# Two attention output projections as seven products of 2x2 blocks, with the tokens on the array's side

## The chip, the cores and the metric

The kernel runs on one NeuronCore of a Trainium2 chip. TensorE (PE) multiplies: a matmul holds a block of 128 x 128 as array weights and streams columns of the other operand through it, at most 512 here. VectorE (DVE), ScalarE (ACT) and GpSimd (POOL) do the elementwise work, SyncE (SP) starts most transfers. Each engine runs its own instructions in order and waits on semaphores for the others. The metric is the device time of one execution in microseconds (us).

## The reference, cut to what matters

A trunk of two layers on 512 tokens of width 1024, all in float32. Layer 0 attends with 8 latent heads of width 128, layer 1 with 16 heads of width 64 over a chunked band; each layer ends with an output projection by a matrix of 1024 x 1024, a norm, a residual sum, and a SwiGLU feed-forward network (FFN).

```python
for layer in range(DEPTH):
    h = rms_norm(x, attn_pre_g[layer])
    y = mla_mixer(h, ...) if layer < N_A_LAYERS else chunked_mixer(h, k_band, v_band, ...)   # each ends: return o @ w_o
    x = x + rms_norm(y, attn_post_g[layer])
    h = rms_norm(x, ffn_pre_g[layer])
    f = swiglu(h, ffn_w_gate[layer], ffn_w_up[layer], ffn_w_down[layer])
    x = x + rms_norm(f, ffn_post_g[layer])
```

`rms_norm(y, g)` is `y * rsqrt(mean(y*y) + 1e-6) * g` over the 1024 features.

## The kernel before

**Layout and precision.** Activations are stored with features on the 128 partitions and the 512 tokens along the row, eight such tiles for width 1024. Each float32 operand is split into a high and a low part: ScalarE casts the high part, VectorE subtracts it to get the low part (`split`, profile lines L144 and L145; with a gain L148 and L149). One product then takes three matmuls: high by high, and the two mixed ones (`mm3`, L352 to L354). In most stages the weights are the array's side and tokens are the moving columns.

**Weights.** `Feed` holds a plan of all weight tiles in order of use. `feed.next` hands out a tile of 1024 columns already split, and keeps up to two later tiles loading through SyncE's queue and splitting. Raw tiles lie in a ring of 5, split tiles (`whi`, `wlo`) in rings of 3; some tiles have rooms of their own (`wh`).

**Attention and what is woven in.** `attention` walks slots of one head and one quarter of the queries. A `Filler` steps a generator of other TensorE work in between, at a rate set by the count `units`; its last part is `out_first`, the first two groups of the output projection, whose last step (k = 7) has to wait for the last head. A head ends when the row sums' reciprocal is spread over the partitions by TensorE (`bc`) and VectorE divides the head (`of`), which is then split (`oh`, `ol`).

**Output projection before.** `out_proj` makes 4 groups of two output blocks over k = 0..7, with W_o as the array's side and the heads as moving columns. Two groups are the woven ones (512 columns), the last two run by halves of 256 tokens, so that the first half's norm can start early. `Post` collects the norm: ScalarE keeps `y` with the gain (L559) and squares, VectorE adds the squares (`acc`), TensorE transposes them (`tot`, L431) for the sums, GpSimd takes the power -1/2 (L448), TensorE spreads the result (`bc`, L465), VectorE multiplies (L597) and adds into `x` (L599). Right behind it `ffn` starts gate/up by token halves (`half`, 256 columns, `b<-xh,whi`).

**Seven products that exist already.** The FFN's down projection (`Down`, `Hidden`, `down`, `After`) is computed with tokens on the array's side and 512 columns of W_down moving (L1169). Tokens, hidden blocks and output columns are each cut in two, and the four blocks of the product come from seven products of sums of blocks, named A11, A22, A12, E1, E2, E3, E6, in place of eight. VectorE or an accumulating DMA of GpSimd's queue (L250) makes the weight sums, VectorE the sums of hidden blocks. Since tokens are then on the partitions, `After` turns the result: ScalarE copies or VectorE adds each product into `y` (L1218, L1223), ScalarE squares with a row sum (L1228), GpSimd takes the power (L1263), ScalarE scales the rows (L1271), TensorE transposes (`yt`, L1291), VectorE adds into `x` with the gain (L1294). After each half of the output columns, `turn(0)` or `turn(1)` does this for the half of the tokens that is whole.

Of the kernel before, what the change touches and what calls it, by code (L numbers as in the profile page):

```python
# [68 lines left out]
def trunk(ctx: ExitStack, tc: tile.TileContext, a, out):  # L69
# [29 lines left out]
    HALF = (slice(0, S // 2), slice(S // 2, S))  # L99
    LO, HI = slice(0, 64), slice(64, 128)  # L100
# [31 lines left out]
    neg = gains[:, G_FPOST[0] * KT:G_FPOST[0] * KT + KT // 2]  # L132
    V.tensor_scalar(neg, neg, -1.0, None, op0=OP.mult)
# [53 lines left out]
    class Down:  # L187
# [7 lines left out]
        TILES = -(-NF // 4)  # L195

        PLAN = {**{s: (3, e) for e, s in enumerate((9, 11, 13, 15, 17, 19))},
                **{s: (4, e) for e, s in enumerate((14, 16, 20, 22, 24, 26))}}

        def __init__(self, src):  # L200
            self.src, self.at = src, {}

        @staticmethod
        def width(i):
            return min(1024, NF // 2 * S - i * 1024)

        def load(self, j, i):
            if j in (self.A11, self.A22):
                self.fetch(j, i, 3 if j else 0, (("raw",) * 5 + ("sum",), ("sum", "sum2", "sum2", "u", "u", "u"))[j][i])
            elif j == self.A12:  # L210
                self.fetch("a21", i, 2, "h")
                self.fetch(j, i, 1, "u")

        def fetch(self, to, i, q, tag):
            n, src = self.width(i), self.src[q, i]
# [22 lines left out]
        def sums(self, j, i):  # L238

            j, e = self.PLAN.get(self.TILES * j + i, (None, 0))  # L240
# [5 lines left out]
            elif j == self.E2:  # L246
                self.plus(j, e, self.E1, self.A11)
                t = self.at[self.E6, e] = self.at[self.A12, e]
                for c, p in enumerate(t):
                    nc.gpsimd.dma_start(p, self.at[j, e][0][:, c * S:c * S + S], accum_op=OP.add)  # L250

    class Feed:
# [14 lines left out]
        def add_down(self, src):  # L267
            d = Down(src)
            for j in range(7):
                for i in range(d.TILES):  # L270
                    self.plan.append((d, d.width(i), (j, i), None))

        def load(self, i):
            while len(self.raw) <= min(i, len(self.plan) - 1):
                src, n, j, _ = self.plan[len(self.raw)]
                if isinstance(src, Down):
# [11 lines left out]
        def split(self, i):  # L288
            while len(self.ready) <= min(i, len(self.plan) - 1):
# [3 lines left out]
                for f in range(j, min(j + 8, len(self.plan))):  # L293
                    if f < j + 5 and isinstance(self.plan[f][0], Pair) or isinstance(self.plan[f][0], Down):
                        self.load(f)
                if isinstance(src, Down):
# [85 lines left out]
    class Filler:  # L382


        def __init__(self, gen):
            self.gen, self.marks, self.end, self.scored = gen, set(), False, False
# [122 lines left out]
    def attention(n_heads, start, fill, first, units, after):  # L509
# [12 lines left out]
        for i in range(slots + 3):  # L522
# [11 lines left out]
            if i >= 6 and i % NQT == 2:  # L534
                t = heads.pop((i - 6) // NQT)
                late.append(t.pv(*t.pt))
            if 2 <= i < slots + 2:
# [8 lines left out]

    class Post:
        def __init__(self, gain, make=U, eps=None, op=OP.add):

            self.gain, self.make, self.sum, self.y, self.r = gain, make, Sum(make), [], {}  # L550
            self.eps, self.op = eps, op

        def rstd(self, ss, h):
            return rstd(ss, D, EPS if self.eps is None else self.eps[:, 2 * h:2 * h + 2])

        def keep(self, b, k, c):
            if len(self.y) <= k:
                self.y.append(self.make(name="y"))
            nc.scalar.activation(self.y[k][:, c], b, AF.Copy, scale=g(self.gain, k))  # L559

        def add(self, b):
            self.keep(b, len(self.y), ALL)
            self.sum.add(b)

        def half(self, h, k, banks):
            for b in banks:
                self.sum.add(b[:, HALF[h]], h)
            for i, b in enumerate(banks):
                self.keep(b[:, HALF[h]], k + i, HALF[h])

# [1071 lines left out]
```

## Time and profile before

| | |
|---|---|
| three runs | 1138.34, 1139.24, 1140.72 us; median 1139.24 |
| profiled execution, its own time | 1138.44 us |
| its span, first to last instruction | 1136.7 us |
| TensorE, VectorE, ScalarE, GpSimd busy | 1114.3, 934.5, 682.0, 65.0 us |
| mean granted TensorE clock | 0.998 |
| bytes moved | 149.80 MB |

The span and the busy times are of the profiled execution, on whose own time the sum below is made. Busy time of TensorE has pipelined matmuls with modelled ends: how fast they follow one another is read from the chain, not from their mean length.

### The profile page before, as it was taken

Reading aid. Unit: us, or ns where it says so; the run is one execution under the profiler, and the core shown is the slowest. Engines: PE = TensorE matmul, PEld = TensorE weight load, DVE = VectorE, ACT = ScalarE, POOL = GpSimd, SP = SyncE. Lnnn points to the kernel's source line nnn. Section 1 sums busy time; section 2 is a strip of 40 time slices with the busy share of each in tenths; the row PEclk is TensorE's granted clock in tenths of the full one; section 3 lists DMA queues with packets and bytes.
Section 4 is the critical chain, followed back from the end, with each engine's and each line's share of the span. In section 5 each row is a group of like instructions: output and inputs, shape, how many; then the busy total and the mean of one; then the engine's idle time right before and its main releaser. Section 6 shows DMA issues by size and latency. Waiting matters only on the chain.

```text
span 1136.7 us, 18969 instructions
## 1 busy us (share of the span) xinstructions
PE 1114.3 (98%) x6973; PEld 989.2 (87%) x6973; DVE 934.5 (82%) x1675; ACT 682.0 (60%) x1335; POOL 65.0 (6%) x90
## 2 busy tenths in 40 slices
PE   9999999999999999999999999999999999999996
PEld 6888889999999998787888888789999999997785
DVE  7788738999899889879758887648999899889867
ACT  6476637645555566578437766656755555566574
POOL 0200000000000002400000000001000000003300
PEclk9999999999999999999999999999999999999999
DMA  7333125422323349932456656534322323359902
GB/s 233 112 107 98 52 94 184 145 79 93 128 81 96 134 148 261 217 97 71 164 149 164 156 165 155 156 119 161 130 75 93 131 93 104 111 178 257 203 2 75
DMA packets 62414, 149.80 MB, mean 132 GB/s; under 512 B 8368, under 2 KB 10160, under 8 KB 62320
## 3 DMA queue, kind: packets, MB, share of 16 engines
q1 hardware_dynamic: 55840, 137.00, 38.5%
q0 software_dynamic: 6336, 11.54, 6.0%
q8 instruction: 55, 0.90, 0.3%
q14 instruction: 39, 0.32, 0.1%
q10 hardware_dynamic: 144, 0.04, 0.0%
HBM read 119.52 MB, written 8.59 MB: 113 GB/s over the span
## 4 chain that ended last, share of the span: by engine, by line
PE 86%; DVE 7%; ACT 3%; DMA 2%; issue 1%; POOL 1%; SPq 0%; DVEq 0%; POOLq 0%; ACTq 0%
PE al L1376 18%; PE b L352 11%; PE b L353 10%; PE b L354 10%; PE be L1376 9%; PE al L1169 8%; PE ga L1376 5%; PE be L1169 3%; PE pt L504 2%; PE de L1169 2%; DVE wlo L145 2%; PE ga L1169 1%; ACT whi L144 1%; DMA x<-mid 1%; PE b L1500 1%
## 5 line engine op out<-in xcount | busy, mean ns | idle before, releaser
L144 ACT CAST whi<-raw 128x1024 fp32r<-128x1024 f32 (+3 forms) x224 | 225.3, 1006 | 217.7 <-PE al L1376 74.8
L145 DVE TENSOR_TENSOR wlo<-raw,whi 128x1024 fp32r<-128x1024 f32 (+3 forms) x224 | 260.5, 1164 | 68.4 <-ACT whi L144 65.8
L1376 PE MATMUL al<-th,whi 128*128 128x256 f32 x432 | 124.1, 287 | 0.1
L1376 PE MATMUL al<-tl,whi 128*128 128x256 f32 x432 | 122.2, 283 | 0.0
L1376 PE MATMUL al<-th,wlo 128*128 128x256 f32 x432 | 122.1, 283 | 0.0
L352 PE MATMUL b<-xh,whi 128*128 128x512 f32 (+1 forms) x304 | 115.7, 383 | 1.3 <-ACT xh L148 1.3
L353 PE MATMUL b<-xl,whi 128*128 128x512 f32 (+1 forms) x304 | 113.0, 372 | 0.0
L354 PE MATMUL b<-xh,wlo 128*128 128x512 f32 (+1 forms) x304 | 112.7, 371 | 0.0
L174 DVE TENSOR_TENSOR raw<-raw,raw 128x1024 f32<-128x1024 f32 x72 | 86.6, 1217 | 2.1 <-DMA raw<-in_w_pair 2.0
L1376 PEld LDWEIGHTS al<-th,whi 128*128 128x128 f32 x432 | 82.7, 192 | 2.1 <-DVE ut L1388 0.4
L1376 PEld LDWEIGHTS al<-th,wlo 128*128 128x128 f32 x432 | 82.8, 192 | 0.0
L1376 PEld LDWEIGHTS al<-tl,whi 128*128 128x128 f32 x432 | 82.8, 192 | 0.0
L492 ACT ACTIVATE p<-p,mn 128x128 f32<-128x128 f32 (+1 forms) x96 | 53.9, 562 | 31.7 <-DVE mn L490 31.4
L145 DVE TENSOR_TENSOR ptl<-pt,pth 128x128 fp32r<-128x128 f32 (+1 forms) x96 | 46.2, 485 | 28.3 <-ACT pth L144 22.7
L352 PEld LDWEIGHTS b<-xh,whi 128*128 128x128 f32 x304 | 57.3, 189 | 9.4 <-ACT xh L148 2.6
L354 PEld LDWEIGHTS b<-xh,wlo 128*128 128x128 f32 x304 | 57.4, 189 | 8.8
L144 ACT CAST whi<-wd 128x512 fp32r<-128x512 f32 x86 | 49.8, 619 | 24.8 <-PE de L1169 8.6
L353 PEld LDWEIGHTS b<-xl,whi 128*128 128x128 f32 x304 | 57.6, 189 | 7.3 <-DVE xl L149 0.7
L145 DVE TENSOR_TENSOR wlo<-wd,whi 128x512 fp32r<-128x512 f32 x86 | 56.2, 684 | 8.3 <-ACT whi L144 7.9
L144 ACT CAST pth<-pt 128x128 fp32r<-128x128 f32 (+1 forms) x96 | 40.2, 423 | 28.7 <-PE pt L504 28.0
L1169 PE MATMUL al<-whi,ph 128*128 128x512 f32 x132 | 51.7, 392 | 0.0
L1169 PE MATMUL al<-whi,pl 128*128 128x512 f32 x132 | 51.6, 391 | 0.0
(304 smaller groups left out, 3269.7 us busy)
## 6 DMA issues: line engine op xcount, KB each, us to landing
raw<-in_w_pair SPq DMA_DIRECT2D x72, 512.0 KB, 3.6
wd<-in_w_down SPq DMA_DIRECT2D x54, 256.0 KB, 5.9
raw<-in_w_o SPq DMA_DIRECT2D x16, 512.0 KB, 3.7
raw<-in_w_gu SPq DMA_DIRECT2D x16, 512.0 KB, 3.7
raw<-in_w_down SPq DMA_DIRECT2D x16, 512.0 KB, 4.4
raw<-in_w_qkb SPq DMA_DIRECT2D x16, 512.0 KB, 3.6
wd<-in_w_down POOLq DMA_DIRECT2D x22, 256.0 KB, 5.8
wd<-raw POOLq DMA_DIRECT2D x22, 256.0 KB, 5.3
```

Source lines behind the costliest of these rows:

```text
L144: return (nc.scalar.copy(dst_hi, src), V.tensor_tensor(dst_lo, src, dst_hi.bitcast(F32), op=OP.subtract))
L145: V.tensor_tensor(dst_lo, src, dst_hi.bitcast(F32), op=OP.subtract))
L174: V.tensor_tensor(t, x, y, op=OP.add)
L352: nc.tensor.matmul(o, l[0], r[0], start=start, stop=False)
L353: nc.tensor.matmul(o, l[0], r[1], start=False, stop=False)
L354: nc.tensor.matmul(o, l[1], r[0], start=False, stop=stop)
L492: nc.scalar.activation(p[:, :n], p[:, :n], AF.Exp, bias=mn[:, :1], scale=-1.0, accum_out=self.sums[:, qt:qt + 1])
L504: nc.tensor.transpose(t[:, kt * P:(kt + 1) * P], p[:, kt * P:(kt + 1) * P], ident)
L1169: nc.tensor.matmul(to[e], l[c], r[d], start=j < 4 and k == 0 and n == 0, stop=k == NF // 2 - 1 and n == 2, skip_group_check=True)
L1376: nc.tensor.matmul(o, l[c], r[d], start=first_ and n == 0, stop=k == K2 - 1 and n == 2, skip_group_check=True)
L1500: nc.tensor.matmul(o[:, q_], vv, pth[:, kt, q_], start=kt == 0, stop=False)
```

## The change

Both output projections become seven products in the manner of the down projection, by the same code. `Down`, `Hidden` and `down` turn into general `Seven`, `Rows` and `seven`; `After` into a base for both uses, with the down projection's special parts in `AfterDown`. `Post`, `out_proj`, `out_first` and `plan_out` are gone. Tokens of two halves are the two row blocks, even and odd heads the two k blocks (4 pairs; in layer 1 a block is a pair of heads of 64), the 512 columns of a half of W_o the moving side.

```diff
+    def out_weights(src):
+        return Seven(src, KT, (Seven.A11, Seven.A22, Seven.A12, Seven.E2, Seven.E3, Seven.E1, Seven.E6),
+                     {Seven.A11: ("raw",) * 2, Seven.A22: ("raw",) * 2, Seven.A12: "uu", "a21": "uu"},
+                     {3: (Seven.E1, 0), 4: (Seven.E1, 1), 5: (Seven.E2, 0), 6: (Seven.E2, 1)}, 4)
...
+    class Rows:
...
+            V.tensor_tensor(m[0], u[:, A0], u[:, A1], op=OP.subtract)
+            V.scalar_tensor_tensor(m[1], m[0], -1.0, v[:, A1], op0=OP.mult, op1=OP.subtract)
+            V.scalar_tensor_tensor(m[3], m[1], -1.0, v[:, A0], op0=OP.mult, op1=OP.subtract)
+            V.tensor_tensor(m[2], v[:, A1], u[:, A1], op=OP.subtract)
...
+    def seven_mm(o, j, k, pairs, l, r):
+        for n, (c, d) in enumerate(((0, 0), (0, 1), (1, 0))):
+            nc.tensor.matmul(o, l[c], r[d], start=j < 4 and k == 0 and n == 0, stop=k == pairs - 1 and n == 2,
+                             skip_group_check=True)
...
+    class Out:
...
+        def first(self):
+            late = []
+            for n, (j, tag) in enumerate(((Seven.A11, "mm"), (Seven.A22, "s"), (Seven.A12, "mm"))):
+                while n and not (fill.scored if n == 1 else fill.weighed):
+                    yield False
...
+                        if n and k == KT // 2 - 1:
+                            late.append(step())
+                        else:
+                            yield from step()
...
+        def rest(self, post):
+            self.rows.at = 3 * self.w.tiles
+            self.banks[Seven.E1] = [bank("s", "be") for _ in range(2)]
+            seven(self.rows, self.w, 3, ((0,), (1,)), post, self.banks)
...
-    attention(H_A, start_a, fill, 13, 8 + 5 * 7 + 6 + 14, False)
+    attention(H_A, start_a, fill, 13, 8 + 5 * 7 + 6 + 6, False)
...
-        post = Post(G_APOST[i], H)
-        last = out_proj(osp, KT, post, firsts, 2)
-        sx = Split(x, G_FPRE[i], H)
-        xs = sx.xs
+        post = After(G_APOST[i], None, H)
+        post.x = fetch(x_src)
+        sx = post.split = Split(post.x, G_FPRE[i], H)
+        oo.rest(post)
+        x, xs = post.x, sx.xs
...
         rest = half(0)
-        post.apply(x, 0, sx.each)
-        post.add_half(1, last, rest, 12, 10)
+        some(rest, 18)
+        post.turn(1)
         run(rest)
         sx.squares(0)
-        post.apply(x, 1, sx.each)
         run(half(1))
...
         def during(self, j, i):
...
+            if j == Seven.E1 and i == 0:
+                while self.later:
+                    self.later.pop(0)()
+            if j == Seven.E6 and i == 0:
                 self.turn(0)
```

The woven part is now A11 whole, A22 up to k = 2 and A12 up to k = 2; their k = 3 waits for the last pair of heads. `rest` does E2, E3 (both on top of A11's banks), E1 and E6. E1's weights are a21 + A22 and E2's E1 + A11 (VectorE); E3's and E6's are added to by accumulating DMAs. w_o is laid out in quarters beforehand, outside the kernel's time, as W_down is. The gain's second half is negated for the signs that the products leave.

A scheduler sets the final order on each engine. Three places show it. In the names, a number tells one tile from another of the same name, "waits" the engines or DMA queues waited for; line numbers of after differ from before's by a few (L146 is the cast L144, L147 the lo part L145, L151 the lo part L149, L661 the product).

ScalarE in layer 0, from the last head's cast on. Before, `oh` is that cast, `b` are banks of the woven groups and `raw` the next weights:

```order
L144 CAST oh_1866<-of_1858 128x512 [waits DVE_49]
L559 ACTIVATE y_1926<-b_1628,gains 128x512 [waits PE_49]
L418 ACTIVATE acc_1928<-b_1628 128x512
L559 ACTIVATE y_1942<-b_1629,gains 128x512 [waits PE_49]
L421 ACTIVATE sq_1944<-b_1629 128x512
L144 CAST wh_1949<-raw_1819 128x512 [waits DMAHW2_49]
L144 CAST whi_2169<-raw_1947 128x1024 [waits DMAHW4_49]
L144 CAST wh_1951<-raw_1819 128x512
L559 ACTIVATE y_1969<-b_1775,gains 128x512 [waits PE_49]
L421 ACTIVATE sq_1971<-b_1775 128x512
L559 ACTIVATE y_1986<-b_1776,gains 128x512 [waits PE_49]
L421 ACTIVATE sq_1988<-b_1776 128x512
```
After, `of_1862` is the last head, `os` are sums of head blocks, `b_1797` and `b_1798` are A22's banks, `whi_1977` is the second weight tile of E2:

```order
L146 CAST ph_1647<-of_1862 128x256 [waits DVE_49]
L146 CAST ph_1643<-os_1638 128x256 [waits DVE_49]
L1146 COPY y_1955<-b_1797 128x512 [waits PE_49]
L146 CAST ph_1965<-os_1078 128x512
L1146 COPY y_1957<-b_1798 128x512 [waits PE_49]
L1150 ACTIVATE sq_1960,ss_471_1930<-y_1951 128x512 [waits DVE_49]
L1150 ACTIVATE sq_1963,ss_471_1930<-y_1953 128x512 [waits DVE_49]
L146 CAST ph_1969<-os_1636 128x512
L146 CAST whi_1977<-raw_1317 128x1024
```
Where keeping `y` and squaring once alternated with casts of W_o (`wh`, `whi_2169`), two copies, two squares and two head casts now stand ahead of that weight cast.

VectorE in layer 0, as the second half's norm comes near. Before, `bc_2121` is the first half's spread factor, `sq_2135` and `sq_2138` are the squares of the last two blocks' second half:

```order
L145 TENSOR_TENSOR wlo_2376<-raw_2291,whi_2375 128x1024 [waits DMAHW2_49,Activation_49]
L597 TENSOR_TENSOR y_1926<-y_1926,bc_2121 128x256 [waits PE_49]
L597 TENSOR_TENSOR y_1942<-y_1942,bc_2121 128x256
L599 TENSOR_TENSOR x_1886<-x_1886,y_1926 128x256 [waits DMAHW0_49,DVE_49]
L422 TENSOR_TENSOR acc_1928<-acc_1928,sq_2135 128x256 [waits Activation_49]
L599 TENSOR_TENSOR x_1888<-x_1888,y_1942 128x256 [waits DVE_49]
L422 TENSOR_TENSOR acc_1928<-acc_1928,sq_2138 128x256 [waits DVE_49,Activation_49]
L597 TENSOR_TENSOR y_1969<-y_1969,bc_2121 128x256
```
After, `y_2021` and `y_2023` are the second half's rows to which E6's banks (`be`) are added, `wh_2222` and `wh_2224` the lo parts of gate/up weights, `ssv` the mean square:

```order
L1212 SCALAR_TENSOR_TENSOR x_1947<-yt_2204,gains,x_1947 128x256 [waits DMAHW1_49]
L151 SCALAR_TENSOR_TENSOR xl_2196<-x_1941,gains,xh_2195 128x256 [waits Activation_49]
L147 TENSOR_TENSOR wh_2222<-raw_2115,wh_2221 128x512 [waits DMAHW2_49]
L151 SCALAR_TENSOR_TENSOR xl_2201<-x_1943,gains,xh_2200 128x256 [waits Activation_49]
L147 TENSOR_TENSOR wh_2224<-raw_2115,wh_2223 128x512 [waits Activation_49]
L151 SCALAR_TENSOR_TENSOR xl_2211<-x_1945,gains,xh_2210 128x256 [waits Activation_49]
L1148 TENSOR_TENSOR y_2021<-y_2021,be_1949 128x512
L151 SCALAR_TENSOR_TENSOR xl_2216<-x_1947,gains,xh_2215 128x256 [waits Activation_49]
L1148 TENSOR_TENSOR y_2023<-y_2023,be_1950 128x512
L1176 TENSOR_SCALAR ssv_1932<-ss_471_1931 128x2
L147 TENSOR_TENSOR wlo_2320<-raw_2219,whi_2319 128x1024 [waits DMAHW5_49]
L1180 SCALAR_TENSOR_TENSOR ssv_1932<-ss_471_1930,ssv_1932 128x2 [waits DVE_49,Activation_49]
```
The first half's additions to `x` and its `xl` now precede the second half's additions to `y`; a lo part of 1024 columns stands between the two steps of `ssv`.

TensorE in the first gate/up half of layer 0, where the second half's norm comes in. Before, `tot` is the transposition of the squares (k = 3 of gate/up around it):

```order
L352 MATMUL b_2208<-xh_2231,wh_2201 128x256
L353 MATMUL b_2208<-xl_2232,wh_2201 128x256
L431 MATMUL tot_2313<-ident,acc_1928 128x128 [waits DVE_49,PE_49]
L431 MATMUL tot_2313<-ident,acc_1928 128x128
L354 MATMUL b_2208<-xh_2231,wh_2202 128x256
L352 MATMUL b_2209<-xh_2231,wh_2201 128x256
```
After, `wh_2285` are gate/up's weights of k = 4 and `y_2021`, `y_2023` the scaled rows:

```order
L363 MATMUL b_2258<-xh_2185,wh_2224 128x256
L361 MATMUL b_2255<-xh_2195,wh_2285 128x256 [waits Activation_49]
L362 MATMUL b_2255<-xl_2196,wh_2285 128x256
L361 MATMUL b_2256<-xh_2195,wh_2285 128x256
L362 MATMUL b_2256<-xl_2196,wh_2285 128x256
L361 MATMUL b_2257<-xh_2195,wh_2285 128x256
L362 MATMUL b_2257<-xl_2196,wh_2285 128x256
L361 MATMUL b_2258<-xh_2195,wh_2285 128x256
L362 MATMUL b_2258<-xl_2196,wh_2285 128x256
L1209 MATMUL yt_2329<-ident,y_2021 128x128 [waits PE_49,Activation_49]
L1209 MATMUL yt_2340<-ident,y_2021 128x128 [waits PE_49]
L363 MATMUL b_2255<-xh_2195,wh_2286 128x256 [waits DVE_49]
```
Before, no scaled rows were turned within gate/up's first half. Now the transposes `yt` stand among the matmuls of k = 4, which they hold up if they are late; and those matmuls' weights are cast on ScalarE behind the squares of `y_2021` and `y_2023`.

512 lines of the change are left out of this document (209 added, 303 removed).

## Prediction

> **What bounds the kernel now.** I read the page's busy shares first, then TensorE's own waits, then the chain, and last the stretches that the change rewrites.
>
> ```profile
> span 1136.7 us, 18969 instructions
> PE 1114.3 (98%) x6973; PEld 989.2 (87%) x6973; DVE 934.5 (82%) x1675; ACT 682.0 (60%) x1335; POOL 65.0 (6%) x90
> ...
> PE 86%; DVE 7%; ACT 3%; DMA 2%; issue 1%; POOL 1%; SPq 0%; DVEq 0%; POOLq 0%; ACTq 0%
> ```
>
> TensorE works 98% of the span and carries 86% of the chain. The list of TensorE's waits (line waited for, total, times, longest) is short; these are its three largest entries:
>
> ```profile
> PE be L1169 <- ACT ph L144: 1.7, 1, 1.7
> PE bc L465 <- POOL r L448: 1.5, 2, 0.8
> PE b L352 <- ACT xh L148: 1.3, 1, 1.3
> ```
>
> So a matmul taken away is worth its full time only if TensorE finds the next one ready. Whether it does is read in the stretches, which the view by windows gives (length; then busy time of PE, PEld, DVE, ACT, POOL; granted clock; DMA share):
>
> ```profile
> 164.70:191.90 27.20, 26.37 (x211) 25.55 (x210) 19.15 (x37) 18.29 (x38) 1.75 (x1) 1.00 0.71 242
> 191.90:238.10 46.20, 46.20 (x302) 42.03 (x301) 44.79 (x104) 30.59 (x63) 2.97 (x2) 1.00 0.28 98
> 737.40:758.30 20.90, 19.27 (x103) 15.67 (x102) 9.23 (x21) 9.23 (x23) 0.00 (x0) 1.00 0.10 29
> 758.30:786.00 27.70, 26.45 (x201) 24.88 (x202) 19.26 (x39) 18.00 (x37) 1.54 (x1) 1.00 0.69 238
> ```
>
> The first row runs from the last head's division to the first gate/up matmul of layer 0, the second from there to the first product of the FFN; the fourth is layer 1's counterpart of the first. In the projection TensorE idles 27.20 - 26.37 = 0.83 us and 27.70 - 26.45 = 1.25 us, about 1.0 a layer. In the gate/up stretch VectorE is busy 44.79 of 46.20 us: whatever VectorE work is pushed into its start will be late.
>
> **TensorE's saving.** Rates come from the chain, where matmuls stand end to end (start, length, what):
>
> ```profile
> 513.81 10.88 PE be L1169 x48
> ...
> 241.17 2.88 PE al L1376 x24
> ...
> 524.70 0.87 PE yt L1291 x8
> ```
>
> 512 columns cost 10.88/48 = 0.227 us, 256 columns 2.88/24 = 0.120, a transpose 0.87/8 = 0.109. A layer's projection had 96 matmuls of 512 columns and 192 of 256: 21.8 + 23.0 = 44.8 us. It now has 7 products x 4 k x 2 output blocks x 3 = 168 of 512: 38.1 us, so -6.7. It gains 24 transposes net (32 more to turn the rows, 8 fewer for sums of squares and their spreading): +2.6. Net **-4.1 us a layer**, -8.2 in all; if all of it landed, the profiled run's 1138.4 would become 1130.2.
>
> The Trainium skill, "TensorE: Matmul & The Clock Gate", section "Back-to-back issue gap", gives an isolated gap of N/2.4 + 2.5 ns, that is 216 ns and 109 ns. By these the matmuls would save 41.6 - 36.3 = 5.4 us a layer and the whole would come out 2.6 us later than by the rows; the trace has 227 and 120 ns.
>
> **What VectorE and ScalarE get instead.** Durations by group (shape, count; busy, mean ns; idle before):
>
> ```profile
> L145 DVE TENSOR_TENSOR wlo<-raw,whi 128x1024 fp32r<-128x1024 f32 x198 | 241.0, 1219 | 63.3 <-ACT whi L144 61.1 <-PE b L354 1.0 <-DMA raw<-in_w_down 0.5
> L144 ACT CAST whi<-raw 128x1024 fp32r<-128x1024 f32 x198 | 207.9, 1050 | 199.6 <-PE al L1376 74.8 <-PE be L1376 32.5 <-issue 29.6
> L145 DVE TENSOR_TENSOR wlo<-wd,whi 128x512 fp32r<-128x512 f32 x86 | 56.2, 684 | 8.3 <-ACT whi L144 7.9
> L144 ACT CAST whi<-wd 128x512 fp32r<-128x512 f32 x86 | 49.8, 619 | 24.8 <-PE de L1169 8.6 <-PE al L1169 8.3 <-PE be L1169 2.6
> L145 DVE TENSOR_TENSOR pl<-hd,ph 128x256 fp32r<-128x256 f32 x66 | 24.6, 416 | 0.4 <-ACT ph L144 0.3
> L1294 DVE SCALAR_TENSOR_TENSOR x<-yt,gains,x 128x256 f32<-128x256 f32 x16 | 6.9, 475 | 0.0
> L149 DVE SCALAR_TENSOR_TENSOR xl<-x,gains,xh 128x256 fp32r<-128x256 f32 x32 | 14.7, 480 | 0.4 <-ACT xh L148 0.4
> L1223 DVE TENSOR_TENSOR y<-y,be 128x512 f32<-128x512 f32 x4 | 2.6, 678 | 0.7 <-PE be L1169 0.7
> L1228 ACT ACTIVATE sq<-y 128x512 f32<-128x512 f32 x16 | 10.0, 626 | 10.7 <-DVE y L1223 10.7
> L1218 ACT COPY y<-al 128x512 f32<-128x512 f32 x8 | 4.7, 585 | 1.8 <-PE al L1169 1.8
> L1271 ACT ACTIVATE y<-y,r 128x512 f32<-128x512 f32 x8 | 5.3, 714 | 1.0 <-POOL r L1263 1.0
> ```
>
> Over both layers VectorE loses 28 lo parts of 512, 80 operations of 256 (`y*bc`, `x+y`, `acc`) and 6 sums of 512: 28 x 0.684 + 80 x 0.416 + 6 x 0.68 = 57 us. It gains 32 turned-row additions (15.2), 32 head sums of 256 (14.3), 32 lo parts of 256 and 12 of 512 (21.5), weight sums (4 of 1024, 8 of 512: 10.4), weight lo parts (6 of 1024, 24 of 512: 23.7) and 16 additions to `y` (10.9): 96 us. Net about +39 us, or 19 a layer, on an engine that is busy 82%. I charge nothing for it as a total, since in most places TensorE's own work covers it. The price lies where it stands ahead of something that TensorE waits for.
>
> **Where TensorE will wait.** Queue steps are taken at the spacing at which operations follow each other, which is 0.07 to 0.08 us under the means above: in the chain four row scales take 2.57, that is 0.64 each against 0.714. The whole existing turn after a `seven` product is in the trace, at the end of layer 0's FFN (the chain, then TensorE's timeline with idle time and releaser in brackets):
>
> ```profile
> 532.96 0.60 DVE y L1223
> ...
> 535.81 0.08 DVE ssv L1261
> ...
> 536.02 1.08 POOL r L1263
> ...
> 537.13 2.57 ACT y L1271 x4
> ```
>
> ```profile
> 530.22 0.39 PE L1169 MATMUL be<-whi,pl 128*128 128x512 f32 x1
> ...
> 531.68 0.50 PE L353 MATMUL b<-wlo,xh 128*128 128x512 f32 x1 [0.61 <-DVE wlo L149]
> ...
> 535.20 0.50 PE L353 MATMUL b<-wlo,xh 128*128 128x512 f32 x1 [0.47 <-DVE wlo L149]
> ...
> 539.75 0.44 PE L1291 MATMUL yt<-ident,y 128*128 128x128 f32 x2 [0.32 <-ACT y L1271]
> ```
>
> From E6's last matmul (end of its slot at 530.45) to the last-waited turned row (539.75) it takes 9.3 us. With the order of instructions shown with the change, four places in layer 0 count; layer 1 has the same order.
>
> 1. *Last head to A12 and A22, k = 3.* Behind the spread VectorE does: division 0.60, a weight lo part 1.14, three head sums (0.40 + 0.34 + 0.40), the lo part 0.34: 3.2 us. TensorE has 10 matmuls ready, 2.3 us. Wait: **1.0**.
> 2. *E2's first two weight tiles.* On ScalarE two copies (0.50 each), two squares (0.55 to 0.62) and two head casts (0.53 each) stand ahead of the cast of E2's second weight tile (0.95), whose lo part (1.14) follows on VectorE behind `ssv`, itself behind the squares. From the last A22 matmul on, I count waits of 0.3 (first cast behind the copy), 0.3 (its lo part behind two additions to `y`), 0.3 (second weight tile) and 0.7 (its lo part): **1.6**.
> 3. *E6 and the first half's turn*, whose scales come while E6's first tile runs: **0.3**, between 0 and 0.7.
> 4. *The second half's turn.* It has to wait for E6's last matmul. TensorE then has 4 transposes and 48 gate/up matmuls, 0.4 + 48 x 0.12 = 6.2 us, before the first matmul on the weights of k = 4. VectorE, starting some 2.5 us before E6's end, has 8 additions of turned rows and 7 `xl` (15 x 0.40), one lo part of 1024 (1.14) and two of 512 (1.2) to do before the additions to `y`: these run from +5.8 to +7.4. The second square ends at +8.0, and only behind it stands the cast of k = 4's weights, done at +8.6: wait 2.4. VectorE's `ssv` falls behind another lo part of 1024 and ends at +8.7, the power at +9.8 (1.08), the second scale at +11.1, the fourth at +12.4; TensorE reaches their transposes at +9.6 and +11.9: waits 1.5 and 0.5. **4.4**.
>
> The sum is 7.3 us a layer. It takes the place of the 1.0 us of idle time that the projection has now; and 0.4 comes from attention's end, where fewer firsts' matmuls fill the last head's waits (the third window idles 1.63 us already). A layer: -4.1 + 7.3 - 1.0 + 0.4 = **+2.6**; both: +5.2. On 1138.4 that gives **1143.6 us**. The median of the runs is 0.8 us above the profiled run, inside their scatter, so I leave it out.
>
> Bounds. Below: place 4 has at least the existing turn's 9.3 against 7.2 us of cover (56 matmuls of 256 and 4 transposes), 2.1 us, and the others could be nothing: -4.1 + 2.1 - 1.0 = -3.0 a layer, 1132.4 us. Above: with full means instead of spacings the places come to about 1.4, 2.6, 1.0 and 6.2, together 11.2: -4.1 + 11.2 - 1.0 + 0.4 = +6.5 a layer, 1151.4 us.
>
> The sums E3 and E6 of the weights are made by accumulating DMAs:
>
> ```profile
> L250 POOL DMA_DIRECT2D wd<-raw x22 | 19.2, 874 | 26.2 <-DMA x<-mid 7.3 <-ACT ph L144 3.9 <-ACT sq L1228 2.8
> ...
> wd<-raw POOLq DMA_DIRECT2D x22, 256.0 KB, 5.3
> ```
>
> Four issues and the landing take 4 x 0.87 + 5.3 = 8.8 us; they are issued over 15 us ahead of use, so nothing is charged. The 2x2 order of w_o moves the same bytes on SyncE's queue.
>
> **Rivals.** *Faster: place 4 costs only the known turn.* It decides at a sum of 4.7 us a layer over the four places: below that the saving survives (-4.1 + 4.7 - 1.0 + 0.4 = 0). For it: the existing turn leaves TensorE only 0.61 + 0.47 + 0.32 us idle. Against it: VectorE there has no 8 additions of a first half and no `xl` of the same half in front. At the lower bound 1132.4 us; chance 0.26.
>
> *Slower: both queues take full durations* because each step waits for a result and not for the queue: 1151.4 us, chance 0.17. *The accumulating DMAs come late* by one landing, 5.3 us a layer: 1143.6 + 10.6 = 1154.2, chance 0.04.
>
> *The clock falls.* After the last matmul the trace shows a fall:
>
> ```profile
> 1128.00:1136.70 8.70, 0.00 (x0) 0.00 (x0) 4.58 (x10) 1.05 (x4) 1.48 (x2) 0.70 0.33 121
> ```
>
> In 8.70 us without a matmul the granted clock averages 0.70; were the low step one half, it would have come after some 3.5 us. If place 4's three waits ran into one gap of that size, and matmuls then ran for as long at half rate, about 1.8 us a layer would be added: 1147.2. My longest single wait is 2.4 us, and TensorE's longest now is 1.7, so 0.03. The Trainium skill, same page, section "HAM oscillation — how this bites in real kernels", asks for no idle gaps over about 3.4 us; the tail's row agrees with it.
>
> That the change would not do what it says is excluded: the matmul counts above are those of the new instruction order.
>
> **The numbers.** The forecast case (its own range 1139 to 1148) has chance 0.50. Range: 1132 to 1153; outside are the late DMAs and a saving below the bound. A measurement of this kernel can tell about 0.2%, 2.3 us, from no change. Faster by more: 0.27 (the first rival). Same: 0.12, the forecast case's lower edge. Slower: 0.61.
>
> **What would show it.** Right: PE busy down by about 8 us, DVE up by some 39; TensorE waits for `whi`/`wlo` at E2, for `wh` at k = 4 and for the scaled `y` at the second turn, 2 to 3 us at the longest, and the largest entry of its list a ScalarE one. Wrong: those waits together under 4.7 us a layer (faster), or waits on `wd` landings, or a granted clock under 1.00 behind E6.

## The result and the profile after

The changed kernel takes **1171.80 us** (median of four runs, 1171.14 to 1174.42) against 1138.79 beside it, a ratio of 1.0292 (95% interval in brackets, here and below) [1.0271, 1.0314]. The sign was as forecast, the size not: 33 us slower where 5 were forecast, outside the range. The profiled execution took 1172.23 us. Its page, the span and the busy shares:

```profile
span 1170.5 us, 18810 instructions
PE 1124.7 (96%) x6781; PEld 984.1 (84%) x6781; DVE 968.2 (83%) x1729; ACT 710.6 (61%) x1397; POOL 80.6 (7%) x106
```

TensorE has 192 fewer instructions and is yet 10.4 us longer busy. So something makes its matmuls longer, and most of that is the granted clock. The view by windows shows where (length; busy PE, PEld, DVE, ACT, POOL, where PEld is TensorE's loading of array weights; granted clock; DMA share; GB/s). Of before: attention of layer 0 up to the last head's spread of the reciprocals, projection with gate/up, the products of the FFN up to layer 1's first row sum, then the same stages of layer 1.

```profile
60.00:164.30 104.30, 103.58 (x581) 88.48 (x579) 70.58 (x161) 61.63 (x145) 0.00 (x0) 1.00 0.26 76
164.30:238.10 73.80, 72.97 (x514) 67.98 (x514) 63.94 (x140) 49.08 (x100) 4.72 (x3) 1.00 0.44 151
238.10:621.40 383.30, 380.05 (x2415) 342.76 (x2414) 327.02 (x516) 225.37 (x410) 23.13 (x30) 1.00 0.47 139
621.40:758.30 136.90, 133.91 (x720) 108.43 (x718) 99.78 (x234) 88.95 (x221) 1.59 (x11) 1.00 0.54 137
758.30:832.20 73.90, 72.65 (x501) 66.87 (x502) 64.01 (x141) 48.47 (x100) 4.54 (x3) 1.00 0.44 150
832.20:1127.70 295.50, 294.16 (x2007) 271.15 (x2005) 260.24 (x388) 172.62 (x299) 20.13 (x23) 1.00 0.43 124
```

The same stages of after (three matmuls of the FFN, 0.4 us, lie ahead of the FFN's edge in each layer):

```profile
60.00:163.50 103.50, 99.70 (x544) 84.08 (x542) 79.40 (x185) 63.42 (x153) 6.21 (x7) 0.97 0.32 85
163.50:251.60 88.10, 82.26 (x456) 70.42 (x454) 72.65 (x143) 62.96 (x126) 6.49 (x5) 0.96 0.44 140
251.60:636.30 384.70, 379.85 (x2408) 341.66 (x2408) 325.87 (x512) 224.02 (x409) 22.80 (x30) 1.00 0.48 138
636.30:773.00 136.70, 129.06 (x677) 102.34 (x675) 108.77 (x261) 88.82 (x227) 8.32 (x19) 0.99 0.59 145
773.00:863.00 90.00, 82.00 (x452) 70.91 (x452) 72.80 (x144) 63.33 (x125) 5.86 (x4) 0.94 0.41 135
863.00:1161.50 298.50, 294.54 (x2004) 270.75 (x2003) 259.16 (x386) 172.07 (x300) 20.09 (x23) 1.00 0.43 122
```

Attention issues 37 and 43 fewer matmuls and takes 0.8 and 0.2 us less. Projection with gate/up takes 14.3 and 16.1 us longer, with 5.0 and 6.7 us more idle time (length less PE busy) and a clock of 0.96 and 0.94. The FFNs, whose mathematics the change leaves alone, take 1.4 and 3.0 us longer. In us, with the matmuls counted by shape in both traces between these edges and taken at the prediction's rates (0.227, 0.120 and 0.109 us; the FFNs' -1.4 are 9 matmuls that lie on the other side of an edge or are missing in a trace), idle time from these rows, and clock lost = (1 - granted clock) x length, summed over windows of 4 us:

| | attention 0 | proj. + gate/up 0 | attention 1 | proj. + gate/up 1 | two FFNs | sum | forecast |
|---|---|---|---|---|---|---|---|
| matmuls and transposes at full rate | -8.4 | +4.4 | -8.2 | +5.2 | -1.4 | -8.4 | -8.2 |
| idle | +3.1 | +5.0 | +4.7 | +6.7 | +4.2 | +23.7 | +13.4 |
| clock lost | +3.4 | +3.4 | +1.7 | +5.1 | 0 | +13.7 | 0 |
| rest (what is left; rounding, and matmuls that do not follow each other at these rates) | +1.1 | +1.5 | +1.6 | -0.9 | +1.6 | +4.8 | 0 |
| longer by | -0.8 | +14.3 | -0.2 | +16.1 | +4.4 | +33.8 | +5.2 |

The first row holds what the forecast did not split: the change takes some 8.3 us of matmuls out of each attention stage and adds 4 to 5 us of them behind it. The forecast's idle time is 2 x (7.3 - 1.0 + 0.4). The list of TensorE's waits (line, releaser; total, times, longest) begins as forecast, with ScalarE's results:

```profile
PE b L661 <- ACT ph L146: 10.0, 8, 3.4
PE yt L1209 <- ACT y L1190: 5.2, 3, 2.5
PE b L361 <- ACT wh L146: 3.3, 2, 1.6
PE sc L1423 <- DVE mn L499: 1.9, 3, 1.4
PE sc L985 <- ACT kh L146: 1.9, 1, 1.9
```

**Place 4 in layer 0.** TensorE's timeline (start, length, what, idle time before and releaser):

```profile
195.86 0.39 PE L661 MATMUL be<-whi,pl 128*128 128x512 f32 x1
...
204.01 0.38 PE L361 MATMUL b<-xh,wh 128*128 128x256 f32 x1 [1.64 <-ACT wh L146]
...
207.68 0.69 PE L1209 MATMUL yt<-ident,y 128*128 128x128 f32 x2 [2.46 <-ACT y L1190]
...
210.72 0.41 PE L361 MATMUL b<-xh,wh 128*128 128x256 f32 x1
210.93 0.41 PE L362 MATMUL b<-xl,wh 128*128 128x256 f32 x1
```

The two waits end 3.7 us apart, in the order forecast: first the weights of k = 4, then the scaled rows, 11.6 us behind E6's last slot. What was not forecast stands in the last two rows: the matmuls follow each other at 0.21 us where the full rate is 0.12. Windows of 4 us show the clock:

```profile
204.00:208.00 4.00, 1.53 (x10) 1.33 (x11) 1.70 (x2) 1.71 (x3) 2.21 (x1) 0.87 0.73 211
208.00:212.00 4.00, 4.00 (x20) 4.00 (x19) 2.11 (x5) 3.26 (x9) 0.00 (x0) 0.50 0.32 123
212.00:216.00 4.00, 4.00 (x29) 4.00 (x29) 3.39 (x10) 3.55 (x11) 0.00 (x0) 0.78 0.97 303
```

The clock stays at one half for two stretches of about 3.4 us, 3.4 us lost. The same happens in layer 1, and single or double stretches follow the waits at 111, 757 and 783 us.

**Layer 1's E2.** The longest wait, in TensorE's timeline:

```profile
778.58 0.93 PE L661 MATMUL b<-whi,pl 128*128 128x512 f32 x3
782.86 0.50 PE L661 MATMUL b<-whi,ph 128*128 128x512 f32 x1 [3.35 <-ACT ph L146]
```

And ScalarE's timeline of that time:

```profile
779.06 1.05 ACT L146 CAST whi<-raw 128x1024 fp32r<-128x1024 f32 x1 [1.69 <-PE b L661]
780.01 1.06 ACT L1146 COPY y<-b 128x512 f32<-128x512 f32 x2
780.97 0.64 ACT L1150 ACTIVATE sq<-y 128x512 f32<-128x512 f32 x1
...
782.20 0.61 ACT L146 CAST ph<-os 128x512 fp32r<-128x512 f32 x1
```

The cast of the head sums for E2 stands in ScalarE's queue behind a weight cast, both copies of A22 and both squares.

### The profile page after: what moved, and what is told of

It reads as the page before. It is cut to its first block, busy times and chain, and to the rows that moved or that the text cites. A ratio compares the mean times of both kernels' runs of the same rounds, so it can differ in the third digit from the quotient of the medians.

```text
span 1170.5 us, 18810 instructions
## 1 busy us (share of the span) xinstructions
PE 1124.7 (96%) x6781; PEld 984.1 (84%) x6781; DVE 968.2 (83%) x1729; ACT 710.6 (61%) x1397; POOL 80.6 (7%) x106
## 5 line engine op out<-in xcount | busy, mean ns | idle before, releaser
L146 ACT CAST whi<-raw 128x1024 fp32r<-128x1024 f32 (+3 forms) x230 | 231.5, 1007 | 231.9 <-PE al L1307 78.4
L147 DVE TENSOR_TENSOR wlo<-raw,whi 128x1024 fp32r<-128x1024 f32 (+3 forms) x230 | 268.3, 1167 | 69.5 <-ACT whi L146 68.6
L661 PE MATMUL b<-whi,ph 128*128 128x512 f32 x388 | 154.3, 399 | 10.0 <-ACT ph L146 10.0
L661 PE MATMUL b<-wlo,ph 128*128 128x512 f32 x388 | 152.9, 395 | 0.6 <-DVE wlo L147 0.5
L661 PE MATMUL b<-whi,pl 128*128 128x512 f32 x388 | 152.1, 397 | 1.3 <-DVE pl L147 0.9
L661 PEld LDWEIGHTS b<-whi,ph 128*128 128x128 f32 x388 | 73.6, 190 | 28.2 <-ACT ph L146 13.5
L661 PEld LDWEIGHTS b<-whi,pl 128*128 128x128 f32 x388 | 73.3, 189 | 20.2 <-DVE pl L147 5.3
L661 PEld LDWEIGHTS b<-wlo,ph 128*128 128x128 f32 x388 | 73.4, 189 | 17.1 <-DVE wlo L147 3.1
L146 ACT CAST whi<-wd 128x512 fp32r<-128x512 f32 x110 | 63.8, 619 | 32.1 <-PE b L661 27.1
L147 DVE TENSOR_TENSOR wlo<-wd,whi 128x512 fp32r<-128x512 f32 x110 | 72.1, 686 | 12.8 <-ACT whi L146 12.3
```

The lines of the kernel that those rows point to most:

```text
L146: return (nc.scalar.copy(dst_hi, src), V.tensor_tensor(dst_lo, src, dst_hi.bitcast(F32), op=OP.subtract))
L147: V.tensor_tensor(dst_lo, src, dst_hi.bitcast(F32), op=OP.subtract))
L661: nc.tensor.matmul(o, l[c], r[d], start=j < 4 and k == 0 and n == 0, stop=k == pairs - 1 and n == 2, skip_group_check=True)
```

## Experiments

The theory that was tested: attention was not bound by TensorE's total but by its own chain, so that taking matmuls from under it leaves holes; the order waits of places 1 to 4 cost their length, and where they gather the clock falls and costs as much again; the rest is the FFN's generalised code. The rivals are told with each run. Ratios are to before; microseconds "against after" are differences of medians.

**1. Attention's rate.** Fewer moved matmuls are woven in at the count of 6; this spreads the work by 14, as before the change.

```diff
-    attention(H_A, start_a, fill, 13, 8 + 5 * 7 + 6 + 6, False)
+    attention(H_A, start_a, fill, 13, 8 + 5 * 7 + 6 + 14, False)
-    attention(H_B, start_b, fill, 12, 7 * 16 + 6, True)
+    attention(H_B, start_b, fill, 12, 7 * 16 + 14, True)
```

> Only the fill rate of attention changes: both calls of attention get 14 again where the change has 6, so woven work is stepped as fast as before the change. Theory (the lower rate lets queries and keys of the next heads come late, TensorE idles, the clock falls): the 1.9 us wait at layer 0's fourth head and the fall of the clock behind it go, 1.9 + 3.4 us, and layer 1's heads lose some 3 of their 4 us of extra idle time and the 1.7 us of low clock: about 1163 us. Rival (attention is bound by its own chain, and less woven work is simply missing): the waits move to the last heads, 1172 within 2 us.

1166.09 us, 1.0239 [1.0210, 1.0269]: 5.7 less than after. TensorE's timeline has the wait that was to go:

```profile
111.50 0.49 PE L985 MATMUL sc<-kh,qh 128*128 128x128 f32 x2 [2.09 <-ACT kh L146]
```

So the rate matters, though not by that wait; attention came out at 101.2 and 133.8 us (103.5 and 136.7 in after). In layer 0 the idle time is that of after, and 1.7 of the 2.3 us are one stretch of low clock fewer; in layer 1 idle time falls by 2.1 us.

**2. E2's casts earlier.** In `seven`, ahead of the copies and squares of the first products:

```diff
+        at = first_ * w_.tiles
+        if first_:
+            rows.ahead(at + 1)
+            feed.ahead(1)
         for j in order[:first_]:
             post.product(j, to[j])
```

> Only the order of code at the start of E2 changes: the casts and lo parts for E2's first two tiles are written ahead of the copies, additions and squares of A11, A22 and A12. Theory: layer 1's wait of 3.35 us before E2's second tile on ScalarE's queue goes with the low clock behind it (1.7 us), and 0.5 us in layer 0: about 1166.5 us. Rival (the squares' results are late then, and the first half's norm takes over the wait): within 2 us of 1172.

1169.04 us, 1.0262 [1.0245, 1.0279], 2.8 less, about half of what was expected. Layer 1's wait of 3.35 shrinks to 1.16, and no fall of the clock follows it:

```profile
779.53 0.50 PE L661 MATMUL b<-whi,ph 128*128 128x512 f32 x1 [1.16 <-ACT ph L146]
```

**3. E6's product first in the queues.**

```diff
+                elif j == Seven.E6 and self.make is not U:
+                    with first(80):
+                        self.put(o, h, banks)
+                        self.rstd(1)
+                    continue
```

> Only the priority of E6's additions to y, squares and power in the projections changes, so that VectorE does the two additions some 8 operations earlier. Theory (VectorE's queue delays the second half's norm): the scaled rows come 3 to 5 us earlier, the 1.6 + 2.4 us of waits at k = 4 shrink below 1 a layer, and the clock no longer falls there (3.4 us a layer): about 1159 us. Rival (the displaced xl and turned-row additions are then late themselves): waits move to k = 1 to 3, 1169 or more.

1168.14 us, 1.0252 [1.0231, 1.0272], 3.7 less and near the rival's 1169. Counted from the last head, 1.1 us earlier here, the additions run 6.1 us earlier (193.82 us in place of 201.02), yet the scaled rows come 0.4 us later: the squares now wait on ScalarE, the mean square behind a lo part, and the power takes 2.82 us. The wait has moved up the queue, not gone (0.83 + 2.21 us in place of 1.64 + 2.46), and the clock is low for one stretch in place of two:

```profile
200.12 0.74 PE L363 MATMUL b<-xh,wh 128*128 128x256 f32 x4 [0.83 <-DVE wh L147]
...
206.98 0.44 PE L1214 MATMUL yt<-ident,y 128*128 128x128 f32 x2 [2.21 <-ACT y L1195]
```

**4 and 5. The clock at place 4.** Transposes of the squares, whose results nobody uses, fill the wait: 16 in front of the scaled rows (`e4_warm`), then 14 tied behind k = 4's last matmul (`e10_warm2`).

```diff
+                if h and not k and self.make is not U:
+                    for n in range(16):
+                        q = n % 4 * P
+                        nc.tensor.transpose(t[:, q:q + P], self.sq[:, q:q + P], ident)
```

> TensorE gets 16 transposes of a tile of squares (0.11 us each, 1.75 us a layer) just ahead of the second half's transposes, into a bank that those overwrite; they stand in the gap and compute nothing that is used. Theory (the low clock is set off by TensorE's idle time at this place and costs on its own): the rows' wait keeps its end, but the clock stays at 1.00 there in both layers, 3.4 us less each: about 1165 us. Rival (the clock falls for another reason, or the extra transposes delay the gate/up matmuls as much): within 2 us of 1172.

> The changed kernel with 14 transposes of a tile of squares a layer (1.5 us) tied behind the last matmul on the weights of k = 4 and ahead of the scaled rows' transposes, in the bank that those overwrite; they lie in the wait for the rows and, unlike the 16 of the run before, push no gate/up matmul behind it. Theory (the low clock costs on its own, 1.7 us for each window of low clock, and chopping the idle time keeps it up): no clock under 1.00 behind the k = 4 waits in either layer, the 3.4 us there saved in each, less up to 0.6 us for a row that is now waited for earlier: 1165 to 1167 us. Rival (at half the clock the matmuls were not the bound there): within 2 us of 1171.8, though the clock stays up.

1170.23 us (1.0283 [1.0252, 1.0314]) and 1175.01 us (1.0314 [1.0297, 1.0330]). The first keeps the clock at 1.00 there and loses 5.1 us of it in place of 13.7, but the scheduler put the 3.5 us of added transposes among the matmuls of k = 4, where they waited themselves (1.15 us for the squares); it is 1.6 us faster. In its trace the stages of projection with gate/up are 1.8 and 3.0 us shorter, with 1.75 us of transposes more, 1.2 of idle time less, and 3.4 and 5.1 of lost clock less; by these figures a us of lost clock is worth some 0.7 us, an estimate. The second keeps one stretch of low clock behind k = 4 in layer 0 and none in layer 1, loses 8.5 us of clock in all, and is 3.2 us slower all the same. In its trace the two stages with the added transposes are 0.8 and 0.3 us shorter, but layer 1's attention is 2.5 us longer: it begins with a wait of 2.75 us (1.02 in after) and a fall of the clock, for a reason that was not tried. So both runs changed more than the clock at this place, and neither isolates its price.

**6 and 7. Is attention bound by its chain?** On the *old* kernel, four steps of the projection's first groups are held back until the last scores are done:

```diff
-                        while len(rhs) <= k:
+                        while len(rhs) <= k or k > 2 and not fill.scored:
```

The counts go from 14 to 6, so this run changes two things. And on the new one (with the rate of 14), 24 matmuls with zero weights per layer are woven into A11:

```diff
+                            if j == Seven.A11 and k < 3:
+                                for e in range(2 if k == 0 else 3):
+                                    for _ in range(3):
+                                        nc.tensor.matmul(b[e % 2], none, w(k % 2 * S, S)[0], start=False, stop=False,
+                                                         skip_group_check=True)
+                                    yield True
```

> The kernel before, with one thing moved: of the woven first group, the steps for k = 3 to 6 (8 steps, 24 matmuls of 512 columns, 5.4 us a layer) wait until the last scores are done, and the fill rate is the change's (6 for 14). No work is added or removed. Theory (attention needs woven work to fill its own waits; taking work away from it doesn't shorten it): the last heads' divisions stay within 2 us of 164.3 and 758.3, so the moved 5.4 us a layer are paid behind it, with some falls of the clock of 1.7 us each: 1149 to 1157 us. Rival (attention is bound by TensorE's work): the last heads end 5.4 us earlier, 1139 within 2 us.

> The changed kernel with the fill rate of before (14) and 24 extra matmuls of 512 columns a layer (5.4 us, 10.9 in all), woven into attention behind A11's steps; their array weights are zero, so they add nothing to A11's sums. To be read against the changed kernel with the rate alone, 1166.1 us. Theory (attention waits for its own chain and the extra matmuls fall into those waits, which also holds the clock up): 1160 to 1167 us, no fall of the clock in attention. Rival (TensorE's work sets attention's length): 1166 + 11 = 1177 us.

Windows of attention, of the old kernel with the steps held back:

```profile
60.00:170.20 110.20, 106.47 (x578) 89.72 (x578) 70.18 (x160) 61.78 (x145) 0.00 (x0) 0.98 0.24 71
627.20:764.10 136.90, 134.88 (x721) 108.05 (x719) 100.52 (x236) 88.36 (x221) 1.60 (x11) 1.00 0.54 137
```

The held matmuls still run ahead of the last head's division, so this is the same work in another order and cannot show what taking work away does. Layer 0 grows by 5.9 us: idle time goes from 0.7 to 3.7, with the wait of 1.9 us for a cast of keys (`kh`) at 109 us that after has too, and the clock takes 1.7. Layer 1 does not grow. The last scores come 4.8 us later in layer 0 and, from the window's start, 1.3 later in layer 1, where the rival has the heads end earlier. The whole: 1146.48 us, 1.0071 [1.0053, 1.0089], between the two forecasts. Now the new kernel's windows of attention with rate 14 alone (run 1):

```profile
60.00:161.20 101.20, 97.41 (x542) 83.29 (x542) 78.94 (x185) 62.97 (x153) 6.39 (x7) 0.98 0.34 88
633.40:767.20 133.80, 128.23 (x675) 103.12 (x673) 108.26 (x259) 88.94 (x227) 8.42 (x19) 0.97 0.61 148
```

The same with the zero-weight matmuls added:

```profile
60.00:162.90 102.90, 99.80 (x550) 84.93 (x549) 78.50 (x185) 61.96 (x150) 5.48 (x6) 0.98 0.31 82
641.00:772.60 131.60, 129.94 (x698) 104.86 (x696) 108.22 (x261) 88.58 (x226) 7.39 (x18) 1.00 0.60 149
```

Layer 1 computes 23 matmuls *more* and is 2.2 us *shorter*: idle time falls from 5.6 to 1.7 us and the clock stays up. There they fell into waits. In layer 0 the window has only 8 matmuls more, for the added ones pushed others of A22 and A12 out of it, and is 1.7 us longer; those others are paid behind it. The stage of projection and gate/up, of run 1 and of this run:

```profile
161.20:247.60 86.40, 80.57 (x453) 68.83 (x452) 72.20 (x142) 62.39 (x125) 6.33 (x4) 0.98 0.44 141
162.90:253.40 90.50, 83.85 (x472) 73.08 (x471) 73.47 (x144) 63.91 (x126) 7.24 (x5) 0.96 0.45 139
```

That is 1.7 + 4.1 us for 5.4 us of added matmuls in layer 0, so there the rival holds. The whole is 1172.32 us (1.0287 [1.0262, 1.0312]), between the two forecasts again. Nor is layer 1's attention bound at before's length: against before, its window here has 3.5 us of matmuls fewer (9 of 512 columns and 12 of 256) and is 5.3 us shorter. What run 7 shows is that in layer 1 the thinner weaving left waits and low clock which cost as much as the matmuls that were gone; that a chain of attention's own sets its length, neither run shows.

**8 and 9. The generalised down projection.** First the old projections with the new common code of the seven products (cut; against after):

```diff
+    class Post:
...
-        oo.rest(post)
...
+        post = Post(G_APOST[i], H)
+        last = out_proj(osp, KT, post, firsts, 2)
```

> Both projections as before the change (Post, out_proj, the old layout of w_o, the old rate), but the down projections by the change's general code (Rows, seven, AfterDown). Theory (the general code orders the head casts of the down projection later; its new waits of 1.0 to 1.5 us there are some 4.5 us of the loss): about 1143 us. Rival (those waits come from what the new projections leave in buffers and queues): 1139 within 2 us.

1145.67 us, 1.0059 [1.0041, 1.0076], so +6.4 us against the 4.5 expected, from code that computes what it did. TensorE's timeline has three waits that before has not:

```profile
427.80 0.50 PE L768 MATMUL b<-whi,ph 128*128 128x512 f32 x1 [1.48 <-ACT ph L146]
...
1024.67 0.50 PE L768 MATMUL b<-whi,ph 128*128 128x512 f32 x1 [1.49 <-ACT ph L146]
...
1029.09 0.50 PE L768 MATMUL b<-whi,ph 128*128 128x512 f32 x1 [1.01 <-ACT ph L146]
```

ScalarE's timeline shows why. Before:

```profile
423.73 1.06 ACT L144 CAST whi<-raw 128x1024 fp32r<-128x1024 f32 x1 [0.71 <-PE al L1169]
424.69 0.71 ACT L144 CAST ph<-hd 128x256 fp32r<-128x256 f32 x2
426.45 1.06 ACT L144 CAST whi<-raw 128x1024 fp32r<-128x1024 f32 x1 [1.05 <-issue]
```

After, at the same place:

```profile
437.11 1.06 ACT L146 CAST whi<-raw 128x1024 fp32r<-128x1024 f32 x1 [0.71 <-PE b L661]
439.83 1.04 ACT L146 CAST whi<-raw 128x1024 fp32r<-128x1024 f32 x1 [1.66 <-PE b L661]
440.78 1.32 ACT L146 CAST ph<-hd 128x256 fp32r<-128x256 f32 x4
```

Two casts of hidden sums (`ph`) that stood ahead of a weight cast now stand behind it. The weight cast waits 1.66 us for TensorE to free its room, with TensorE's next operand behind it. The one thing that the new code writes differently there is the order of two sums on VectorE:

```diff
+            V.tensor_tensor(m[2], v[:, A1], u[:, A1], op=OP.subtract)
             V.scalar_tensor_tensor(m[3], m[1], -1.0, v[:, A0], op0=OP.mult, op1=OP.subtract)
-            V.tensor_tensor(m[2], v[:, A1], u[:, A1], op=OP.subtract)
```

> The changed kernel with two lines of Rows.add swapped, so that VectorE makes the head sum m[2] ahead of m[3], as the code before did for the hidden blocks; nothing else. With the old projections, this swap puts ScalarE's instructions in the order of before throughout. Theory (the down projections' extra waits come from the order in which two sums are written, through the scheduler's list, and not from the new projections): the new waits of 1.5, 1.5 and 1.0 us in the down projections go, 4.5 to 6 us in all, about 1166.5 us. Rival (what the projections leave behind keeps these waits): within 2 us of 1171.8.

On the changed kernel this gives 1166.34 us, 1.0242 [1.0226, 1.0257], 5.5 less than after; layer 1's FFN is back at before's 295.5:

```profile
862.00:1157.50 295.50, 294.09 (x2007) 271.10 (x2005) 259.35 (x387) 172.32 (x298) 20.08 (x23) 1.00 0.43 124
```

**10 to 12. Together.** First the rate of 14 and E2's early casts, with the weights of gate/up's next tiles asked for ahead of E6's product and the second turn tied behind gate/up's 28th step in place of its 18th:

```diff
+            if first_ and j == order[-1]:
+                feed.ahead(2)
-        some(rest, 18)
-        post.turn(1)
+        for _ in range(28):
+            done = next(rest)
+        post.turn(1, done)
```

> The changed kernel with four edits to its order: the fill rate of before, E2's casts ahead of the squares, gate/up's k = 4 weights split ahead of E6's norm, and the second half's transposes tied behind the 28th of the 32 steps of gate/up's first half (where the change allowed them from the 18th on). Theory (every one of these waits is one of queues and placing): the two waits at k = 4 (1.6 + 2.4 us a layer) shrink to about 1 and the clock stays at 1.00 there, 5 to 6 us a layer, beside 5.7 for the rate and 2.8 for E2: about 1152 us. Rival (the second half's rows are then late for gate/up's second half, which waits in place of the first): 1160 or more.

1160.52 us, 1.0184 [1.0165, 1.0202], 11.3 less, where 1152 was forecast and the rival said 1160 or more. The waits for k = 4's weights are gone and the clock holds at E2 and at k = 4; TensorE still waits 1.5 and 0.8 us a layer for the turned rows. Then with the order of the two sums as well, and last with a rate of 24:

> The four edits of order that gave 1160.5 us together with the two swapped lines. If the parts add up: 1160.5 less 4.5 to 6, about 1155 us. If the swap changes the scheduler's lists elsewhere for the worse, 1158 or more. On either reading it stays above the kernel before, since attention's heads are not shortened by the work taken away from them.

> The same, with 24 in place of 14 as attention's count of woven steps, so that queries and keys of the next heads are stepped earlier. Theory (the head of layer 0 that waits 2 us for its keys and the pairs of layer 1 that starve do so for lack of early work): the wait at 112 us goes and with it 1.7 us of low clock, 1151 us. Rival (the woven work runs out earlier instead and the last heads wait more): 1155 or more.

1156.33 us (1.0155 [1.0140, 1.0171]) and **1153.69 us** (1.0125 [1.0108, 1.0141]). The first is near the sum of the parts, the second between its two forecasts. Windows of the last, attention and projection with gate/up of layer 0, and layer 1's attention:

```profile
60.00:159.90 99.90, 96.61 (x543) 81.66 (x542) 79.45 (x185) 62.46 (x153) 7.28 (x8) 1.00 0.37 92
159.90:242.90 83.00, 78.66 (x453) 67.34 (x452) 71.87 (x141) 62.08 (x125) 3.78 (x3) 1.00 0.43 143
630.00:764.20 134.20, 125.94 (x665) 102.43 (x666) 106.26 (x257) 87.11 (x224) 8.74 (x19) 0.96 0.61 150
```

In layer 0 attention is 4.4 us below before and the wait at 111 us is gone, so here about half of the 8.3 us of matmuls taken out lands. Layer 1's attention is 2.7 us below before in spite of 5.1 us of clock lost in it. Projection with gate/up still takes 9.2 us more than before's 73.8, at full clock: 4.2 are the matmuls that the change moves there and 3.5 are idle time. Edits of order and rate alone took back 18.1 of the 33 us; no version that was run beats before.

## Why the forecast missed

*Right.* The matmuls at full rate went down by 8.4 us by count, against 8.2. The four places, counted by the waits of TensorE's timeline, gave 0.9 + 0.3 + 0.5 + 1.6 + 2.5 = 5.8 us in layer 0 and 0.5 + 3.35 + 1.6 + 2.4 = 7.9 in layer 1, against 7.3 each; the idle time that projection with gate/up gained, 11.7 us, stands against the 12.6 forecast. Place 4's rows came 11.6 us after E6, against 11.1. VectorE is 33.7 us longer busy, against 39.

*Wrong, step "if all of it landed".* The prediction let all of the saving land and charged 0.4 us a layer for attention's thinner filler. Attention got 7.8 us more idle time in the two layers, and the clock took 5.1 there: 16.6 us of matmuls left it and 1.0 us came out, while what the change puts behind attention was paid in full. Run 12 shows that this is no fixed limit: woven at another rate and order, 4.4 us come out in layer 0. Layer 1 stays open, as the clock fell in its attention in every version of the new kernel but run 7's. The waits of before that the prediction quoted at attention's end (1.63 us idle in 20.9) were a sign that TensorE was not alone on the path there, and it took them as the whole price.

*Wrong, the rival "the clock falls".* Its mechanism was right, its place among the rivals not: it was priced at 1.8 us a layer with a chance of 0.03, on the reading that a fall needs 3.5 us without work. The runs show falls after much less. Idle time of at most 1.33 us within 3.4 us was never followed by a fall in these traces; single waits of 1.5 to 1.7 were in some 6 of 35 cases, the same wait in one kernel's trace and not in another's; the wait at some 109 us, 1.88 to 2.10 us long, was in all 11 traces that have it; longer ones mostly were, though two of 3.3 us were not. In after, waits of 1.4 to 3.4 us, each harmless by the prediction's reading, set off falls at five places, and a clock under 1.00 behind E6 is what the prediction had named as a sign of being wrong. The Trainium skill, "TensorE: Matmul & The Clock Gate", section "HAM oscillation — how this bites in real kernels", names gaps of over about 3.4 us; here the measurement decides, and a gap of 2.1 is enough. In after each fall holds for one or two stretches of 3.4 us (up to four in runs 11 and 12) and takes 1.7 us a stretch, 13.7 us in all. What that is worth in time: executions of one kernel differ in their granted clock, and over 52 executions of 13 kernels, each against its own kernel's mean, the span grows by 0.82 +- 0.10 us for each us of clock lost. That makes about 11 of the 33 us. It is a correlation, in which a longer wait and the fall behind it come together; the two runs that were to isolate the price at one place did not, though the first of them gives the estimate of 0.7.

*Wrong, a term that was missing.* The prediction put nothing down for the down projection's move to the common code. Its order changed by one line, and that cost 5.5 to 6.4 us (runs 8 and 9).

*Wrong in part, place 2.* The one count for both layers was 1.6 us; layer 0's waits there came to 0.8, and layer 1 waited 3.35 for a head cast behind five other operations. Run 2 cuts that to 1.16.

*Left over.* The "rest" of 4.8 us has no cause that was tried here. Nor is it settled why layer 0's wait at 111 us outlasts the rate of 14 and goes with 24, though the old kernel has it too once its rate is 6 (run 6 against before).

## What to carry to other kernels

Matmuls that fill other engines' waits may save little when they go: here 8.4 and 8.2 us of them left two attention stages, and 0.8 and 0.2 us came out. Before counting a saving, split it by stage, ask in each what ends last once TensorE has less to do, and set the rate of weaving anew. Price waits in clusters: those of 1.6 and 2.5 us at place 4, some 1.2 us of work apart, were followed by another 3.4 us of lost clock. And code that is "only generalised" is a change too: two lines of equal work in another order moved 5.5 us.

## What was not expected of the hardware

GpSimd's power of two columns, charged at 1.08 us, took 0.71 in the first half's norm and 2.21 in the second's, and 2.82 in run 3. GpSimd's timeline:

```profile
186.16 0.71 POOL L1182 TENSOR_TENSOR r<-ssv,mhalf 128x2 f32<-128x2 f32 x1 [20.96 <-DVE ssv L1180]
204.04 2.21 POOL L1182 TENSOR_TENSOR r<-ssv,mhalf 128x2 f32<-128x2 f32 x1 [17.17 <-DVE ssv L1180]
```

VectorE stood idle from 186.06 to 187.30, during the short one, and ran a lo part of 1024 columns from 203.88 on, during the long one. Over the traces this power of the projections takes 0.71 us wherever VectorE stands idle beside it, 1.95 beside a lo part of 1024 and two additions of 256 (runs 10 to 12), and 2.2 to 2.8 beside one of 1024 and one or two of 512. The Trainium skill, "GPSIMD Engine Reference", section "1. Specifications", has the two engines share their interfaces to the on-chip memory, with contention from some forms of VectorE instructions; the two rows agree with it, but no run varied VectorE's load alone.
